# Weight casts moved in a decoder block: two gate units, two output units, one FFN unit, and two row blocks of the projection summed together

## The chip, the cores and the metric

The kernel runs on one core of a Trainium2 chip. Its time is the device time of one execution in microseconds (us). The engines are named as in the profile: PE (TensorE, matmuls), PEld (its weight loads), DVE (VectorE), ACT (ScalarE), POOL (GpSimd) and SP (SyncE, which here issues the DMAs).

## The reference

One decoder block on x of 1 x 1024 x 1024 floats: a projection, two attentions, gates, an output projection and a SwiGLU FFN of width 2816.

```python
h = rmsnorm(x, mix_norm_g[l])
proj = h @ w_in[l]
qa, ka, va, q_lat, kv_lat, k_r, g_a, g_b = jnp.split(proj, IN_OFFSETS, axis=-1)
...
o_a = swa_sink_attention(qa, ka, va, swa_sinks[l])      # 8 heads, window 128
...
o_b = mla_attention(q_nope, q_rope, k_nope, k_rope, vb) # 8 heads, causal
y = jax.nn.sigmoid(g_a) * (o_a @ w_o_swa[l]) + jax.nn.sigmoid(g_b) * (o_b @ w_o_mla[l])
x = x + y @ w_out[l]
h = rmsnorm(x, ffn_norm_g[l])
x = x + (jax.nn.silu(h @ w_gate[l]) * (h @ w_up[l])) @ w_down[l]
return rmsnorm(x, final_norm_g)
```

## The kernel before

Everything is single precision. A float operand is split in two parts: `split(hi, lo, src)` casts to the narrower type that PE takes (`hi`, on ACT, line 163) and subtracts it from the source (`lo`, on DVE, line 166). `mm3` then makes each product of three matmuls: high by high (line 172), high by low (173) and low by high (174). Nearly every weight passes through such a pair of a cast on ACT and a subtraction on DVE before PE can use it; `wl`, `wh` and `wv` are the names of split weights, `wr` of raw ones, and `pth`/`ptl`, `yh`/`yl`, `t3h`/`t3l` and so on those of split activations.

The stages that the change touches, in the order of the program:

- **Gates and local attention** (scores from 129 to 304 us). The two gate projections are computed by the class `Seven` in seven block products per pair of columns j, each for q in a fixed sequence; `gates.run()` runs the next unit (j, q), and `prep_to(n)` prepares units (additions on POOL, then the split of the weights, `wl`) until n are prepared, by default 3 ahead (`n_ahead`). The loop over `it` interleaves three gate units (`gate_step`) with one block of the sliding-window attention: `sw_qT` transposes and splits the queries (`qs`), `sw_scores` makes the scores (`sc`, lines 917 and 918), their maxima on DVE (921), and the exponentials on ACT (933); `sw_pT` and `sw_pv` multiply by the values (`o`, copied to `ot` at 964). `scale_gate` multiplies raw weights of later units by the norm's gain on ACT (837).
- **The mix** (`oB` from 564 to 610 us). For eight columns `DCS = (4, 5, 0, 1, 6, 7, 2, 3)`, `mix_b` makes `oB`, the product with `w_o_mla`, multiplies it by the gate and adds the other half: `sg<-oB,sg`, `sg<-sg,sg`, then the split into `yh` and `yl`. The weights come as units ("ob", 0..3) of two columns each, through a stream `st` of loads and conversions: `conv_to(i)` emits the conversions up to unit i (ACT `wh`, DVE `wl`). ("ob", 3) is used by columns 6 and 7, ("ob", 1) by 2 and 3.
- **The projection** (`xo`, from 610 us), a row block of 128 and 512 columns at a time: eight products of `y` with `w_out`, in the order of DCS, into one accumulator of the pool P1 (four banks).
- **The FFN's first units** (from about 705 us), again by `Seven`, with units for the gate (g) and the up projection (u); the tail of the projection's transposes (`late_parts`) lies between them.

What sets the order: PE and SP follow the written order in the gate stage and a scheduler orders ACT, DVE and POOL; in the mix the scheduler orders PE too, except that casts and sigmoids emitted while `held[0]` is set keep their place; from the last segment of the projection on, PE, DVE, ACT and POOL all follow the written order. Buffers are taken from pools in the order of emission.

Of the kernel before, what the change touches and what calls it, by code (L numbers as in the profile page):

```python
# [89 lines left out]
def hybrid_block_kernel(  # L90
# [49 lines left out]
    def uid(name):  # L140
        counter[0] += 1
        return f"{name}_{counter[0]}"
# [7 lines left out]
    def tiny(name, w=1):  # L150
        return small.tile([P, w], F32, tag=f"t{w}", name=uid(name))

    def P1(name, shape=(P, 512)):
        return ps1.tile(list(shape), F32, tag="ps", name=uid(name))

    def PX(name, shape=(P, 512)):
        return psum["x"].tile(list(shape), F32, tag="ps", name=uid(name))
# [10 lines left out]
    def mm3(ps, pairs, first=True, last=True, go_on=False):  # L168

        n = len(pairs)  # L170
        for i, ((ah, al), (bh, bl)) in enumerate(pairs):
            nc.tensor.matmul(ps, ah, bh, start=first and i == 0, stop=False, skip_group_check=go_on)  # L172
            nc.tensor.matmul(ps, ah, bl, start=False, stop=False, skip_group_check=go_on)  # L173
            nc.tensor.matmul(ps, al, bh, start=False, stop=last and i == n - 1, skip_group_check=go_on)  # L174
# [7 lines left out]
    def blk(b, n=1):  # L182
        return slice(b * P, (b + n) * P)
# [35 lines left out]
    st = Stream()  # L219
# [102 lines left out]
    def hT(k, sl):  # L322
        hi, lo = quad[(k // 4, sl.start // 512)]
        c = slice(sl.start % 512, (sl.stop - 1) % 512 + 1)
        return hi[:, k % 4, c], lo[:, k % 4, c]
# [193 lines left out]
    ps = kvq_ps[0] = PX("kvq")  # L519
# [337 lines left out]
    gates = Seven(NK, "g", load_gate, gate_done, 3, (1, 6), 5, scale=scale_gate, scale_at=[(2, 0, 0, 2), (7, 0, 2, 2), (7, 1, 0, 2), (5, 1, 2, 2)], piece=2, vec=(2, 5))  # L857
# [6 lines left out]
    for b in range(NB):  # L864
# [4 lines left out]
        ps = PX("ql", (P, 416))  # L869
# [35 lines left out]
    def sw_scores(it):  # L905
        g, b = divmod(it, NB)
        d = sw[it]
        qs = d.pop("qs")
        c0 = P if b == 0 else 0
        kc = slice((b - 1) * P + c0, (b + 1) * P)  # L910
        mx = tiny("mx", 4)
        scs = []
        for hp in range(2):
            sc = PX("sc", (P, 2, 2 * P))
            scs.append(sc)
            for j in range(2):
                nc.tensor.matmul(sc[:, j, c0:], qs[:, hp, j], khd[g][0][:, kc], start=True, stop=False)
                nc.tensor.matmul(sc[:, j, c0:], qs[:, hp, j], khd[g][1][:, kc], start=False, stop=True)
            for j in range(2):
                h = 2 * hp + j  # L920
                nc.vector.tensor_tensor_reduce(sc[:, j, c0:], sc[:, j, c0:], band[:, c0:], 1.0, NEG, op0=ALU.add,
                                               op1=ALU.max, accum_out=mx[:, h:h + 1])
        ns = nsink[:, 4 * g:4 * g + 4]
        nm = tiny("nm", 4)
        nc.vector.scalar_tensor_tensor(nm, mx, -SC_A, ns, op0=ALU.mult, op1=ALU.min)
        es = tiny("es", 4)
        nc.vector.tensor_tensor(es, nm, ns, op=ALU.subtract)
        den = tiny("den", 4)
        pe = U("pe", F32, (P, 4, 2 * P))
        for h in range(4):  # L930
            if h == 1:
                nc.scalar.activation(es, es, AF.Exp)
            nc.scalar.activation(pe[:, h, c0:], scs[h // 2][:, h % 2, c0:], AF.Exp, scale=SC_A, bias=nm[:, h:h + 1],
                                 accum_out=den[:, h:h + 1])
        nc.gpsimd.tensor_tensor(den, den, es, op=ALU.add)
        nc.gpsimd.tensor_tensor(den, den, neg_one, op=ALU.pow)
        for h in range(4):
            nc.gpsimd.tensor_scalar(pe[:, h, c0:], pe[:, h, c0:], den[:, h:h + 1], 0.0, op0=ALU.mult, op1=ALU.add)
        d["pe"] = pe
        d["kbs"] = [1] if b == 0 else [0, 1]  # L940
# [38 lines left out]
    for i, b in enumerate((4, 5, 6, 7, 0, 1, 2, 3)):  # L979
        ps = P1("kl", (P, KVL))  # L980
# [44 lines left out]
    for it in range(N_SW):  # L1025
        if it + 2 < N_SW:
            sw_q(it + 2)
        gate_step()
        if it + 1 < N_SW:
            sw_qT(it + 1)  # L1030
        gate_step()
        if it >= 1:
            sw_pv(it - 1)
        if it + 1 < N_SW:
            sw_scores(it + 1)
        if it == N_SW - 1:
            load_lat(4)
        gate_step()
        sw_pT(it)
# [125 lines left out]
    ob = {}  # L1165
# [145 lines left out]
    DCS = (4, 5, 0, 1, 6, 7, 2, 3)  # L1311
# [99 lines left out]
    def mix_b(dc, i):  # L1411
        if dc % 2 == 0:
            wo[4 + dc // 2] = st.get(("ob", dc // 2))
        w = wo[4 + dc // 2]
        ga, gb = gate.pop(dc), gate.pop(8 + dc)
        for sh in range(2):
            cs = half(sh)
            pb = PX("oB")
            mm3(pb, [((w[0][:, c, blk(dc % 2)], w[1][:, c, blk(dc % 2)]), obT[(c, sh)]) for c in range(4)])
            nc.vector.tensor_tensor(gb[:, cs], pb, gb[:, cs], op=ALU.mult)  # L1420
            if i == 7:
                add(ga[:, cs], ga[:, cs], gb[:, cs], nc.vector)
                split(*hT(dc, cs), ga[:, cs])
        for sh in range(2 if i < 7 else 0):
            cs = half(sh)
            add(ga[:, cs], ga[:, cs], gb[:, cs], nc.vector)
            split(*hT(dc, cs), ga[:, cs])

    def sigmoids(dc):
        for i in (dc, 8 + dc):  # L1430
            sigmoid(i)
        a_ = ar.pop(dc)
        for sh in range(2):
            nc.gpsimd.tensor_tensor(gate[dc][:, half(sh)], a_[:, half(sh)], gate[dc][:, half(sh)], op=ALU.mult)
# [9 lines left out]
    for i, dc in enumerate(DCS):  # L1444
        if i in (1, 2):
            st.load_to(st.index[("ob", (3, 1)[i - 1])])
        if 2 <= i < 6:
            st.load_to(st.index[("out", 0, OUT0[i - 2])])
        if i + 2 < 8:
            load_sigs(DCS[i + 2])  # L1450
        if rest:
            mix_a(*rest.pop(0), 0, 4, PX("oA"))
        if i + 1 < 8:
            sigmoids(DCS[i + 1])
        mix_b(dc, i)
        if i in (2, 3):
            st.conv_to(st.index[("ob", (3, 1)[i - 2])])
        if i >= 4:
            st.conv_to(st.index[("out", 0, OUT0[i - 4])])

# [60 lines left out]
    def ffn_done(j, m, ps, f, sh, other):  # L1521
# [8 lines left out]
        else:  # L1530
# [3 lines left out]
    ffn = Seven(HF, "gu", load_w, ffn_done, 4, (2, 7), 5, head,  # L1534
                {(1, 6): [("load", 2, 0)], (1, 7): [("load", 2, 1)], (1, 5): [("mix", 2)]})
# [75 lines left out]
    for seg, (sh, hf) in enumerate(((0, 0), (0, 1), (1, 1), (1, 0))):  # L1611
        if seg == 3:
            in_order.__enter__()
        if seg in (0, 1, 3):
            r = {0: 0, 1: 1, 3: 2}[seg]
            wo2 = [st.get(("out", r, j)) for j in range(4)]
        hs = half(hf)
        for b in range(4 * sh, 4 * sh + 4):
            if seg in (0, 2):
                x2[b] = load_x(b)  # L1620
            if (seg, b) == (2, 4):
                ffn.load_part(0, 0)
            if (seg, b) == (2, 6):
                ffn.load_part(0, 1)
            if (seg, b) == (2, 7):
                ffn.mix(0)
            ps = P1("xo")
            mm3(ps, [(hT(k, blk(b)), (wo2[k // 2][0][:, k % 2], wo2[k // 2][1][:, k % 2])) for k in DCS])
            add(x2[b][:, hs], ps, x2[b][:, hs], nc.vector)
            if seg in (0, 2):  # L1630
                st.conv_to(st.index[("out", seg // 2 + 1, b % 4)])
            if seg in (1, 3):
                xn = U("xn")
                ss = tiny("ss")
                nc.scalar.activation(xn, x2[b], AF.Square, accum_out=ss)  # L1635
                rs = rstd_of(ss, D)
            lower = to_h(*prev) if prev is not None else None
            prev = None
            if seg in (1, 3):
                nc.vector.scalar_tensor_tensor(xn, x2[b], rs, fg_bc, op0=ALU.mult, op1=ALU.mult)  # L1640
                prev = (xn, b)
                if (seg, b) == (3, 6):
                    ffn.prep_to(3)
                nc.sync.dma_start(x2_d[b], x2.pop(b))
            if (seg, b) == (3, 7):
                for kh in range(2):
                    ffn.load_part(1, kh)
            if lower is not None:
                if seg == 3 and b >= 6:
                    late_parts.append(lower)  # L1650
                else:
                    lower()
# [1 line left out]
    ffn.run()  # L1654
    late_parts.pop(0)()
    ffn.run()
    ffn.prep_to(4)
    late_parts.pop(0)()
    ffn.run()
    ffn.prep_to(6)  # L1660
# [89 lines left out]
    i = 0  # L1750
# [125 lines left out]
```

## Time and profile before

| | |
|---|---|
| median of 3 runs | 1345.6 us (1345.04 to 1346.36) |
| the profiled execution | 1345.58 us, its span 1343.8 us, mean granted clock 0.998 |
| PE busy | 1325.5 us, 99% of the span, 6564 matmuls |
| DVE, ACT, POOL busy | 67%, 47%, 42% |
| DMA | 223.61 MB, mean 166 GB/s |

In the rows of the timeline the columns are start, duration (both us), engine, line, operation, output <- inputs, sizes, and in brackets the idle time of the engine before the row and what released it. A matmul's duration overlaps that of the next one; the distance between starts is what one costs. In the table of waits a row reads: engine, tile and line that waited <- engine, tile and line that released it, then the total, the number of times and the longest.

### The profile page before, as it was taken

How to read it: one execution, taken by the hardware profiler on the slowest of the kernel's cores; microseconds unless marked ns; L12 is line 12 of the kernel's file. 1: busy time of each engine (PE TensorE's matmuls, PEld its weight loads, DVE VectorE, ACT ScalarE, POOL GpSimd, SP SyncE). 2: the span in 40 equal slices, each digit the busy share in tenths (PEclk: the TensorE clock that was granted, in tenths of full speed). 3: DMA queues.
4: the chain of work that ended last, by engine and by line, in shares of the span. 5: the costliest groups of instructions: out<-in, count | busy, mean ns of one | idle time of the engine just before them, and what ended most of it. 6: DMA issues, size and time to landing. Idle time of an engine off the chain costs nothing. (4 is left out here: it accounts for less than half of the span.)

```text
span 1343.8 us, 19035 instructions
## 1 busy us (share of the span) xinstructions
PE 1325.5 (99%) x6564; PEld 1115.0 (83%) x6564; DVE 903.5 (67%) x1471; ACT 635.7 (47%) x1291; POOL 567.6 (42%) x614
## 2 busy tenths in 40 slices
PE   9999999999999999999999999999999999999997
PEld 6899878888888889877887888888888888888886
DVE  7868777776767667696458775566665664764862
ACT  7434767665556767762436223232223232644343
POOL 2116646553224554451031665756666541022521
PEclk9999999999999999999999999999999999999999
DMA  9454322335476430771432454545544425996504
GB/s 374 152 188 156 118 97 83 109 124 187 155 243 160 107 99 17 264 268 48 190 140 96 166 175 146 203 162 180 177 141 153 164 96 194 383 373 238 173 13 144
DMA packets 85311, 223.61 MB, mean 166 GB/s; under 512 B 9632, under 2 KB 16288, under 8 KB 84128
## 3 DMA queue, kind: packets, MB, share of 16 engines
q1 hardware_dynamic: 83776, 220.05, 47.5%
q10 hardware_dynamic: 1440, 2.36, 0.5%
q8 instruction: 52, 0.85, 0.3%
q14 instruction: 43, 0.35, 0.1%
HBM read 151.72 MB, written 70.12 MB: 165 GB/s over the span
## 5 line engine op out<-in xcount | busy, mean ns | idle before, releaser
L166 DVE TENSOR_TENSOR wl<-wr,wl 128x512 fp32r<-128x512 f32 x150 | 150.8, 1029 | 72.6 <-ACT wl L163 72.2
L166 DVE TENSOR_TENSOR lrv<-lr,lrv 128x1024 fp32r<-128x1024 f32 x77 | 105.1, 1396 | 49.3 <-ACT lrv L163 45.3
L163 ACT CAST lrv<-lr 128x1024 fp32r<-128x1024 f32 x77 | 80.1, 1052 | 95.7 <-PE fd L174 69.8
L172 PE MATMUL fd<-lrv 128*128 128x512 f32 x308 | 119.8, 389 | 0.0
L173 PE MATMUL fd<-lrv 128*128 128x512 f32 x308 | 119.8, 389 | 0.0
L174 PE MATMUL fd<-lrv 128*128 128x512 f32 x308 | 119.8, 389 | 0.0
L177 POOL TENSOR_TENSOR wr<-wr,sm 128x512 f32<-128x512 f32 (+1 forms) x38 | 46.2, 1225 | 145.4 <-DVE wl L166 114.2
L163 ACT CAST wl<-wr 128x512 fp32r<-128x512 f32 x150 | 86.9, 622 | 1.9 <-DVE wr L835 1.7
L1198 POOL TENSOR_TENSOR denb<-denb,neg_one 128x1 f32<-128x1 f32 x64 | 40.1, 626 | 96.2 <-ACT p L1197 84.1
L166 DVE TENSOR_TENSOR wl<-sm,wl 128x512 fp32r<-128x512 f32 x60 | 48.7, 837 | 46.3 <-ACT wl L163 46.2
L311 POOL TENSOR_SCALAR ms<-ss 128x1 f32<-128x1 f32 x32 | 9.4, 292 | 143.7 <-ACT xn L1635 67.5
L173 PEld LDWEIGHTS fd<-lrv 128*128 128x128 f32 x308 | 57.8, 188 | 12.1
L174 PEld LDWEIGHTS fd<-lrv 128*128 128x128 f32 x308 | 57.8, 188 | 12.0
L172 PEld LDWEIGHTS fd<-lrv 128*128 128x128 f32 x308 | 57.8, 188 | 11.9
L1197 ACT ACTIVATE p<-scb,nmb 128x384 f32<-128x384 f32 (+3 forms) x64 | 47.8, 747 | 33.3 <-DVE nmb L1196 25.6
L166 DVE TENSOR_TENSOR ptl<-pTb,pth 128x512 fp32r<-128x512 f32 (+2 forms) x96 | 50.5, 552 | 16.6 <-ACT pth L163 16.3
L1196 DVE CUSTOM_DVE_ANT_0 scb<-scb,mask 128x384 f32<-128x384 f32 (+3 forms) x64 | 48.6, 761 | 15.0 <-PE scb L1188 13.0
L1529 ACT ACTIVATE act<-sm 128x512 f32<-128x512 f32 x11 | 7.0, 633 | 104.8 <-DVE sm L180 104.8
L1199 POOL TENSOR_SCALAR p<-p,denb 128x384 f32<-128x384 f32 (+3 forms) x64 | 47.9, 748 | 6.3
L172 PE MATMUL xo<-wv,yh 128*128 128x512 f32 x120 | 47.4, 395 | 1.2 <-ACT yh L163 1.2
L1529 ACT ACTIVATE act<-pu 128x512 f32<-128x512 f32 x22 | 13.9, 633 | 71.0 <-DVE pu L180 71.0
L163 ACT CAST pth<-pTb 128x512 fp32r<-128x512 f32 (+2 forms) x96 | 43.4, 482 | 8.5 <-PE pTb L1213 7.5
(356 smaller groups left out, 4315.1 us busy)
## 6 DMA issues: line engine op xcount, KB each, us to landing
lr<-la_d SPq DMA_DIRECT2D x77, 256.0 KB, 5.4
wr<-in_w_gate_dram SPq DMA_DIRECT2D x22, 512.0 KB, 4.4
wr<-in_w_up_dram SPq DMA_DIRECT2D x22, 512.0 KB, 5.1
wd<-in_w_down_dram SPq DMA_DIRECT2D x22, 512.0 KB, 7.1
rb_d<-wd SPq DMA_DIRECT2D x22, 512.0 KB, 2.7
la_d<-sd SPq DMA_DIRECT2D x22, 512.0 KB, 5.9
lr<-rb_d SPq DMA_DIRECT2D x44, 256.0 KB, 5.4
lr<-in_w_down_dram SPq DMA_DIRECT2D x33, 256.0 KB, 5.4
```

The costliest lines, as they stand in the source:

```text
L163: i = nc.scalar.copy(hi, src)
L166: (eng or nc.vector).tensor_tensor(lo, src, hi.bitcast(F32), op=ALU.subtract)
L172: nc.tensor.matmul(ps, ah, bh, start=first and i == 0, stop=False, skip_group_check=go_on)
L173: nc.tensor.matmul(ps, ah, bl, start=False, stop=False, skip_group_check=go_on)
L174: nc.tensor.matmul(ps, al, bh, start=False, stop=last and i == n - 1, skip_group_check=go_on)
L177: eng.tensor_tensor(out, a, b, op=ALU.subtract)
L311: nc.gpsimd.tensor_scalar(ms, ss, 1.0 / width, EPS, op0=ALU.mult, op1=ALU.add)
L1196: nc.vector.tensor_tensor_reduce(s_, s_, m_, 1.0, -NEG, op0=ALU.add, op1=ALU.min, accum_out=nm)
L1197: nc.scalar.activation(p_, s_, AF.Exp, scale=-1.0, bias=nm, accum_out=den)
L1198: nc.gpsimd.tensor_tensor(den, den, neg_one[:, 0:1], op=ALU.pow)
L1199: nc.gpsimd.tensor_scalar(p[:, 0:w], p[:, 0:w], den, 0.0, op0=ALU.mult, op1=ALU.add)
L1529: nc.scalar.activation(dst, src, AF.Silu)
```

## The change

Four edits. In the loop of the local attention, when the next gate unit to run is (2, 1) or (5, 1), the gates are prepared up to three units ahead already before `sw_scores`. The conversions of ("ob", 3) and ("ob", 1) are called ahead of `mix_b` at i = 2 and 4, instead of behind it at i = 2 and 3. In the projection the first two row blocks take an accumulator each and sum the first six columns of DCS for both, then the last two columns for both. And `ffn.prep_to(4)` becomes `prep_to(5)`.

```diff
         if it + 1 < N_SW:
+            if gates.seq[gates.n_run][:2] in ((2, 1), (5, 1)):
+                gates.prep_to(gates.n_run + 3)
             sw_scores(it + 1)
...
             sigmoids(DCS[i + 1])
+        if i in (2, 4):
+            st.conv_to(st.index[("ob", (3, 1)[i // 2 - 1])])
         mix_b(dc, i)
-        if i in (2, 3):
-            st.conv_to(st.index[("ob", (3, 1)[i - 2])])
...
-            ps = P1("xo")
-            mm3(ps, [(hT(k, blk(b)), (wo2[k // 2][0][:, k % 2], wo2[k // 2][1][:, k % 2])) for k in DCS])
+            if seg == 0 and b < 2:
+                if b == 0:
+                    xo2 = [P1("xo") for _ in range(2)]
+                    for ks in (DCS[:6], DCS[6:]):
+                        for u in range(2):
+                            mm3(xo2[u], [(hT(k, blk(u)), (wo2[k // 2][0][:, k % 2], wo2[k // 2][1][:, k % 2])) for k in ks],
+                                ks[0] == DCS[0], ks[0] != DCS[0])
+                ps = xo2[b]
+            else:
+                ps = P1("xo")
+                mm3(ps, [(hT(k, blk(b)), (wo2[k // 2][0][:, k % 2], wo2[k // 2][1][:, k % 2])) for k in DCS])
...
-    ffn.prep_to(4)
+    ffn.prep_to(5)
```

ACT at the first of the two gate places, before; the first `wl` row is the cast of unit (2, 2), `pe` are the exponentials, `pth` the split of the transposed probabilities:

```order
L964 COPY ot_2304<-o_2299 64x512
L933 ACTIVATE pe_2329,den_2328<-sc_2310,nm_2324 128x256
L932 ACTIVATE es_2326<-es_2326 128x4
L933 ACTIVATE pe_2329,den_2328<-sc_2310,nm_2324 128x256
L933 ACTIVATE pe_2329,den_2328<-sc_2317,nm_2324 128x256 x2
L163 COPY wl_2341<-wr_2089 128x512
L163 COPY pth_2362<-pT_2364 128x512
L163 COPY pth_2362<-pT_2371 128x512
L163 COPY wl_2382<-wr_2025 128x512
L899 COPY qs_2404<-qT_2401 64x2x128
```

And after:

```order
L964 COPY ot_2304<-o_2299 64x512
L163 COPY wl_2309<-wr_2089 128x512
L933 ACTIVATE pe_2332,den_2331<-sc_2313,nm_2327 128x256
L932 ACTIVATE es_2329<-es_2329 128x4
L933 ACTIVATE pe_2332,den_2331<-sc_2313,nm_2327 128x256
L933 ACTIVATE pe_2332,den_2331<-sc_2320,nm_2327 128x256 x2
L163 COPY pth_2362<-pT_2364 128x512
L163 COPY pth_2362<-pT_2371 128x512
L163 COPY wl_2382<-wr_2025 128x512
L837 ACTIVATE wr_2344<-wr_2344,gT 128x256
L899 COPY qs_2404<-qT_2401 64x2x128
```

The cast now stands ahead of the exponentials, and one gain multiplication (837) ahead of `qs`. Behind these rows two more gain multiplications have moved ahead of the next copy to `ot`. On DVE the low half of the cast moved ahead of three of the four maxima.

ACT in the mix, before; `wh_6812` is the cast of unit ("ob", 1), `wv` are casts of `w_out`:

```order
L1269 ACTIVATE sg_6724<-sg_6724 128x1024
L163 COPY yh_6608<-sg_6674 128x512
L163 COPY wh_6812<-wr_6718 128x1024
L163 COPY wv_6911<-wr_6768 128x1024
L1269 ACTIVATE sg_6770<-sg_6770 128x1024
L1269 ACTIVATE sg_6772<-sg_6772 128x1024
L163 COPY yh_6610<-sg_6722 128x512
L163 COPY yh_6612<-sg_6722 128x512
L163 COPY wv_6952<-wr_6816 128x1024
L1269 ACTIVATE sg_6818<-sg_6818 128x1024
```

And after, where the same cast is called `wh_6824`:

```order
L1271 ACTIVATE sg_6724<-sg_6724 128x1024
L163 COPY yh_6608<-sg_6674 128x512
L163 COPY wv_6911<-wr_6768 128x1024
L1271 ACTIVATE sg_6770<-sg_6770 128x1024
L1271 ACTIVATE sg_6772<-sg_6772 128x1024
L163 COPY yh_6610<-sg_6722 128x512
L163 COPY yh_6612<-sg_6722 128x512
L163 COPY wv_6952<-wr_6812 128x1024
L163 COPY wh_6824<-wr_6718 128x1024
L1271 ACTIVATE sg_6814<-sg_6814 128x1024
```

The cast of unit 1 moved behind two sigmoids, two `yh` and a `wv`. That of unit 3, a few rows earlier, stands in the same place in both programs, and so do its low half on DVE and its matmuls on PE.

PE at the first matmuls that use unit 1, after; before, the rows of `oB_6918` ran through without a break:

```order
L172 MATMUL oB_6918<-obT_6206,wh_6824 128x512
L173 MATMUL oB_6918<-obT_6206,wh_6824 128x512
L172 MATMUL oB_6932<-obT_6206,wh_6824 128x512
L173 MATMUL oB_6932<-obT_6206,wh_6824 128x512
L172 MATMUL oB_6955<-obT_6206,wh_6824 128x512
L173 MATMUL oB_6955<-obT_6206,wh_6824 128x512
L172 MATMUL xo_6998<-wv_6862,yh_6610 128x512
L173 MATMUL xo_6998<-wv_6862,yh_6610 128x512
L174 MATMUL xo_6998<-wv_6862,yl_6611 128x512
L172 MATMUL xo_6998<-wv_6862,yh_6610 128x512
L174 MATMUL oB_6918<-obT_6206,wl_6825 128x512
```

Ahead of the first matmul that needs the low half (`wl_6825`) now stand two matmuls of each of three columns' halves and four of the projection.

In the FFN, ACT and DVE follow the written order: the first of the two casts that stood behind the activation (line 1529) now stands directly behind the cast of the unit before it, ahead of `b22h`, `t3h`, the table load and the activation.

## The prediction

> **What bounds the kernel now.** I read the page's busy times first, then the table of waits for TensorE, then the timeline around each wait.
>
> ```profile
> span 1343.8 us, 19035 instructions
> PE 1325.5 (99%) x6564; PEld 1115.0 (83%) x6564; DVE 903.5 (67%) x1471; ACT 635.7 (47%) x1291; POOL 567.6 (42%) x614
> ```
>
> PE is busy for 99% of the span and the change removes no matmul, so all there is to win or lose is PE's idle time. The profiled execution took 1345.58 us, the span and 1.8 us around it; the median of the runs is 1345.6, so I sum against 1345.58. About 0.2%, 2.7 us, is what a measurement of this kernel can tell from no change. The waits of PE (total, times, longest):
>
> ```profile
> PE fa L172 <- ACT wl L163: 3.3, 3, 1.5
> PE xo L172 <- ACT yh L163: 1.2, 1, 1.2
> PE oB L172 <- ACT wh L163: 0.9, 1, 0.9
> PE oB L174 <- DVE wl L166: 0.9, 1, 0.9
> ```
>
> Each edit is aimed at one of these: the gates at two of the three `fa` waits, ffn.prep_to(5) at the third, the projection at `xo`, the earlier `ob` conversion at `oB`. They sum to 6.3 us, 0.5% of the time. A wait costs more than its row. The timeline at the first gate wait shows it:
>
> ```profile
> 196.25 0.39 PE L896 MATMUL qT<-ident,qn 128*128 128x128 f32 x2
> 197.68 0.50 PE L172 MATMUL fa<-hh,wl 128*128 128x512 f32 x1 [1.04 <-ACT wl L163]
> ...
> 198.74 0.39 PE L172 MATMUL fa<-hh,wl 128*128 128x512 f32 x1
> ...
> 596.56 0.39 PE L172 MATMUL oB<-obT,wh 128*128 128x512 f32 x1
> ...
> 599.28 0.39 PE L172 MATMUL oB<-obT,wh 128*128 128x512 f32 x1
> ```
>
> The last two rows are twelve undisturbed `oB` matmuls apart: 2.72/12 = 0.227 us each. From 197.68 to 198.74 PE starts three matmuls in 1.06 instead of 0.68 us: a tail of 0.38. The two transposes at 196.25 take some 0.23, so PE could have gone on at about 196.48: idle 1.2, and 1.58 with the tail.
>
> **The gates.** ACT and DVE around that wait:
>
> ```profile
> 195.09 0.47 ACT L933 ACTIVATE pe<-sc,nm 128x256 f32<-128x256 f32 x1 [3.66 <-DVE nm L925]
> 197.00 0.62 ACT L163 CAST wl<-wr 128x512 fp32r<-128x512 f32 x1
> 202.64 0.59 ACT L964 COPY ot<-o 64x512 f32<-64x512 f32 x1
> 207.62 0.63 ACT L163 CAST wl<-wr 128x512 fp32r<-128x512 f32 x1
> 197.66 0.69 DVE L166 TENSOR_TENSOR wl<-wr,wl 128x512 fp32r<-128x512 f32 x1 [1.80 <-ACT wl L163]
> 201.45 0.42 DVE L902 TENSOR_TENSOR qs<-qT,qs 64x256 fp32r<-64x256 f32 x1
> 208.28 0.69 DVE L166 TENSOR_TENSOR wl<-wr,wl 128x512 fp32r<-128x512 f32 x1 [1.76 <-ACT wl L163]
> 201.72 0.28 PE L917 MATMUL sc<-khd,qs 128*128 128x256 f32 x1
> 209.33 0.47 PE L172 MATMUL fb<-t4h,wl 128*128 128x512 f32 x1
> ```
>
> ACT sat idle for 3.66 us ahead of its exponentials (195.09), and the cast (197.00) stood behind them. In the new order it stands ahead of them, so the wait goes: +1.58. What it adds: DVE's low half of the cast (0.69) now lies ahead of the maxima, so the exponentials start some 0.6 later, near 195.7. The scheduler also puts one gate-gain ACTIVATE ahead of `qs` and two of the next four ahead of the copy to `ot`; four take 1.70 us in one row:
>
> ```profile
> 200.30 1.70 ACT L837 ACTIVATE wr<-wr,gT 128x256 f32<-128x256 f32 x4
> ```
>
> so 0.43 each. The scores (201.72) need `qs`, whose last DVE half starts at 201.45 and whose first comes 0.45 sooner; nothing in the DVE order makes it earlier by more than 0.4. PE would now reach the scores at 201.72 - 1.58 = 200.14 and find the first half done at about 201.1 to 201.5. It waits 1.0 to 1.4 there: 0.2 to 0.6 of the 1.58 is left. Then `ot` (202.64) moves back by about 1.0 (three ACTIVATEs, less the cast that went ahead), the second maxima, exponentials and the cast behind them (207.62, its low half 208.28 to 208.97) with it, against a slack of 0.36 at 209.33. PE waits again, 0.4 to 0.7 with a tail. I take +0.3 us slower for this gate. The second gate has the same rows 79 us later:
>
> ```profile
> 276.76 0.50 PE L172 MATMUL fa<-hh,wl 128*128 128x512 f32 x1 [0.76 <-ACT wl L163]
> ```
>
> with 0.76 of idle by the row, and 0.54 more if the first gate's 1.58 for a row of 1.04 is a guide, so 1.3; by the same steps, 0.2 slower. Both: +0.5 us, from -2.9 (both waits go, nothing new) to +1.2.
>
> **The oB weights.** Rows of the two units whose conversion is moved:
>
> ```profile
> 587.09 0.50 PE L172 MATMUL oB<-obT,wh 128*128 128x512 f32 x1 [0.94 <-ACT wh L163]
> 589.40 0.50 PE L174 MATMUL oB<-obT,wl 128*128 128x512 f32 x1 [0.89 <-DVE wl L166]
> 592.47 1.05 ACT L163 CAST wh<-wr 128x1024 fp32r<-128x1024 f32 x1
> 599.67 0.63 ACT L163 CAST yh<-sg 128x512 fp32r<-128x512 f32 x1 [1.03 <-DVE sg L180]
> 600.20 1.04 ACT L163 CAST wv<-wr 128x1024 fp32r<-128x1024 f32 x1
> 588.13 1.22 DVE L166 TENSOR_TENSOR wl<-wr,wh 128x1024 fp32r<-128x1024 f32 x1
> 594.52 1.72 DVE L166 TENSOR_TENSOR wl<-wr,wh 128x1024 fp32r<-128x1024 f32 x1
> ```
>
> For unit 3 (wait 587.09 and 589.40) the new order of ACT, DVE and PE is the old one there, so these 1.8 us stay. For unit 1 the cast `wh`, at 592.47 before, is emitted one column later, and ACT's order puts it behind two `yh` and a `wv` (the second `yh` at 599.67, `wv` at 600.20). The `yh` wait for DVE's sums, which the edit does not hasten, so `wh` follows `wv` at about 601.2 and, with its 1.05, ends at 602.2. PE wants it at 599.28, the first matmul of the columns 2 and 3. New wait: 602.25 - 599.28 = 2.97, with a tail of 0.38 about 3.4. The low half (1.22 and 1.72 in its two rows) ends near 604.4 to 604.9; PE's new order fills in six `oB` and four `xo` matmuls (10 x 0.227 + 0.38 = 2.65, to 604.9), so it adds 0 to 0.4. Behind `wh` queue two sigmoids and the next `yh`; POOL and DVE wait for those, PE only later.
>
> **The projection.** The first row block waits for the last column:
>
> ```profile
> 616.32 0.50 PE L172 MATMUL xo<-wv,yh 128*128 128x512 f32 x1 [1.24 <-ACT yh L163]
> 615.65 0.62 ACT L163 CAST yh<-sg 128x512 fp32r<-128x512 f32 x1 [1.84 <-DVE sg L180]
> ```
>
> 1.24 by the row, and 0.54 more as at the gates: 1.78. Now the first six columns of two row blocks come first, so 36 matmuls, 32 of them (7.3 us) behind the oB matmuls, stand before the one that needs the last `yh` (cast at 615.65). That wait goes: -1.78. The number of matmuls is unchanged, and two accumulators of four are in use. SP's order is the same, and its late loads feed weights that are used tens of us later. Weights and projection: 3.4 - 1.8 = +1.6 us, from -1.8 (unit 1 hidden) to +2.2.
>
> **The FFN.** Rows around the third `fa` wait:
>
> ```profile
> 718.77 0.50 PE L172 MATMUL fa<-b11h,wl 128*128 128x512 f32 x1 [1.46 <-ACT wl L163]
> 715.20 0.59 ACT L1500 CAST b22h<-tp 128x512 fp32r<-128x512 f32 x1 [1.36 <-DVE t L177]
> 718.11 1.13 ACT L163 CAST wl<-wr 128x512 fp32r<-128x512 f32 x2
> 722.63 0.62 ACT L163 CAST wl<-wr 128x512 fp32r<-128x512 f32 x1
> 715.08 1.41 DVE L177 TENSOR_TENSOR t2l<-t,t2h 128x512 fp32r<-128x512 f32 x1
> 724.62 0.39 PE L172 MATMUL fa<-b21h,wl 128*128 128x512 f32 x1
> ```
>
> The wait is 1.46 by its row, and 0.54 more as at the gates: 2.0. Of the two casts at 718.11 (the gate's unit and the up projection's) the first moves ahead of 715.20, where ACT was idle for 1.36 by that row. Its low half pushes DVE's and ACT's chain back by about 0.6. Then PE arrives 2.0 earlier at the next units. The up unit's cast comes just in time or 0.3 late. The unit after it has its cast at 722.63 behind a chain of transposes, not moved: PE, which reached it at 724.62 before, reaches it at 722.6 and waits until 723.3, 0.7 and a tail: 1.1. Left: 2.0 - 1.1 - 0.2 = 0.7. In this stretch DVE's `t2l` (715.08) took 1.41, where the same shape at the gates took 0.69; POOL works beside it. If the moved low half takes that long, the up unit is 0.7 later and the gain is nil; I take 0.7 since only one of the rows in that stretch is long, and keep 0 to 2.0.
> [...]
>
> **The sum.** +0.5 + 1.6 - 0.7 = +1.4: 1345.58 + 1.4 = 1347.0 us.
>
> **The rivals.** (1) The waits simply go. For it: each cast moves into a row of ACT idle time. Against it: the next consumer of each stage is 0.4 to 1.6 us behind. Gates -2.9, FFN -2.0, weights and projection +1.6: -3.3, 1342.3; if unit 1 is hidden too, -6.7, 1338.9. Chance 0.13.
> (2) Slower: the late `wh` cast of unit 1 decides alone. Every microsecond by which it ends after 602.2 is one more of PE's. The rows at 588.13 and 594.52 show one DVE form at 1.22 and, beside POOL's multiplications, 1.72; three such stretches ahead of the second `yh` end `wh` at 603.7, the wait is 4.9 instead of 3.4, and if the FFN gives nothing the sum is +0.5 + 4.9 - 1.8 = +3.6, 1349.2. It decides from a `wh` end of about 602.8, where the sum passes +2.7 without the FFN's gain. Chance 0.17.
> (3) A wait of 3 us drops PE's clock: rows show only the short tail for waits up to 1.5, none of 3. Were matmuls at half rate for as long as the wait, 3.4/0.45 = 7.5 of them would each cost 0.227 more: +1.7, in all +3.1, 1348.7. Chance 0.06. [...]
> (4) The change does not do what it says: the scheduler has already kept unit 3's cast in its place; if it hides unit 1's as well through timing that the order does not show, and gates and FFN cancel, only the projection is left: -1.8, 1343.8. Chance 0.08.
> My forecast has 0.56.
>
> **Chances and range.** Over 0.2% faster: (1), 0.13. Over 0.2% slower: (2), (3) and the upper end of the forecast: 0.24. Within: 0.63. The range takes the forecast's unknowns (-2.6 to +3.3) takes in the near case of (1) and (2): 1342.2 to 1349.3. Left out are the far case of (1) and ends beyond (2).
>
> **What would show it.** Right: PE waits at `oB` L172 for ACT `wh` twice, the new one 2.5 to 3.5 us; no `xo` wait for `yh`; new short waits at `sc` L917 and at the `fb` and `fa` units behind the moved ones. Wrong: no new `oB` wait, or `fa` waits under 0.5 us in all with no `sc` wait in their place; either would take 2 to 3 us off.

## The result and the profile after

The changed kernel takes 1348.99 us (median of 7 runs, 1348.29 to 1350.26), the kernel before 1345.04 in the runs beside it (7 runs, 1344.72 to 1348.04). The ratio is 1.0027, with a 95% interval of 1.0015 to 1.0038: slower by 2.0 to 5.1 us. Predicted were 1347.0 us and a range of 1342.2 to 1349.3. The profiled execution took 1350.21 us. Its span and busy times on the page:

```profile
span 1348.4 us, 19047 instructions
PE 1330.3 (99%) x6564; PEld 1116.7 (83%) x6564; DVE 903.6 (67%) x1471; ACT 635.6 (47%) x1291; POOL 569.8 (42%) x614
```

The same 6564 matmuls take 4.8 us more of PE time, and the span is 4.6 longer: what was lost is not idle time of PE alone, since matmuls themselves have become slower somewhere. The table of PE's waits after the change:

```profile
PE oB L172 <- ACT wh L163: 3.7, 2, 2.8
PE sc L917 <- DVE qs L901: 1.6, 2, 0.8
...
PE oB L174 <- DVE wl L166: 0.9, 1, 0.9
...
PE fa L172 <- ACT pu L812: 0.2, 1, 0.2
PE fa L172 <- ACT wl L163: 0.2, 1, 0.2
```

The three `fa` waits of before (3.3 in all) have shrunk to two of 0.2, and the `xo` wait (1.2) is gone. In their place stand two waits of 0.8 at the scores, and a second `oB` wait for ACT's `wh`, of 2.8. The waits that the change touches sum to 6.3 us before and to 6.6 after. So 4.6 us of span are not to be found in this table.

To place them, each PE matmul's start in a profile is set against the start of the same matmul in the profile of before. This **shift**, its median over stretches of 20 us, changes only where time is lost or won. From the changed kernel's start to its end it goes 0, 2.3 (from 20 us on), 2.1 (from 150 us on, still ahead of the first edit), 2.7 (behind the two gates), 5.4 (behind the mix and the projection), 4.6 (behind the FFN's first units, and to the end).

**The first 2.1 us** are not the change's: up to there the two programs have the same instructions in the same order. The first projection's 16 matmuls in the timeline of before, and of after:

```profile
5.72 7.10 PE L522 MATMUL kvq<-wr,h 128*128 128x512 f32 x16 [1.11 <-DMA wr<-in_w_x_dram]
```

```profile
5.43 9.70 PE L522 MATMUL kvq<-wr,h 128*128 128x512 f32 x16 [0.60 <-DMA wr<-in_w_x_dram]
```

They take 9.70 instead of 7.10 us. The trace's record of PE's clock reaches full speed 4.27 us into the span of before, and 10.64 us into that of after. Among the profiles of the other kernels below it is 5.1 to 5.4 or 9.9 to 10.4 with the same instructions at the start (4.27 in one), so executions that begin alike differ in this; by the shift of 2.1 it can scatter the times of single runs by about 2 us, an estimate. The shift at a place is free of it. What the change did is therefore 4.6 - 2.1 = 2.5 us in the traces, and the interval of the times, 2.0 to 5.1, holds that.

**The mix: a new wait, and half a clock behind it.** PE's timeline of after at the first matmuls with unit 1's weights:

```profile
601.75 0.39 PE L174 MATMUL oB<-obT,wl 128*128 128x512 f32 x1
604.93 0.79 PE L172 MATMUL oB<-obT,wh 128*128 128x512 f32 x1 [2.79 <-ACT wh L163]
605.52 0.63 PE L173 MATMUL oB<-obT,wh 128*128 128x512 f32 x1
605.95 0.63 PE L172 MATMUL oB<-obT,wh 128*128 128x512 f32 x1
...
607.65 0.55 PE L172 MATMUL xo<-wv,yh 128*128 128x512 f32 x1
```

and ACT's just before, then the windows of the same stretch (columns: window in us, its length, busy us and instructions of PE, PEld, DVE, ACT and POOL, granted clock of PE, DMA share, GB/s):

```profile
601.82 1.17 ACT L163 CAST yh<-sg 128x512 fp32r<-128x512 f32 x2 [3.98 <-DVE sg L180]
602.89 1.04 ACT L163 CAST wv<-wr 128x1024 fp32r<-128x1024 f32 x1
603.84 1.04 ACT L163 CAST wh<-wr 128x1024 fp32r<-128x1024 f32 x1
```

```profile
602.00:605.00 3.00, 0.21 (x2) 0.07 (x1) 3.00 (x6) 3.00 (x5) 0.00 (x0) 0.93 0.87 269
604.90:608.00 3.10, 3.07 (x7) 2.48 (x8) 3.10 (x4) 2.39 (x3) 2.09 (x1) 0.50 0.85 280
608.00:612.00 4.00, 4.00 (x19) 3.30 (x18) 3.22 (x4) 1.57 (x3) 1.85 (x2) 1.00 0.86 331
```

ACT's `wh` stands behind `yh`, `yh` and `wv`, and the first of those waits 3.98 us for DVE's sums, as was worked out. PE starts nothing from 601.75 to 604.93: 3.18 us, of which 0.227 are the last matmul's, so 2.95 are lost. Then the starts are 0.43 apart (605.52, 605.95) instead of 0.227, up to 607.65; the granted clock is 0.50 in that window and 1.00 in the next. The clock record has 0.5 for 3.41 us, from 604.56 to 607.97. Of that, 3.04 us lie behind the wait. From 604.93 to the full clock the matmuls' starts take 1.5 us more than 0.227 us each would: half of the 3.04. That is where PE's busy time grew while the table of waits stayed as long.

**The gates.** ACT, DVE and PE at the first gate, by start:

```profile
193.45 0.62 ACT L163 CAST wl<-wr 128x512 fp32r<-128x512 f32 x1
197.95 0.47 ACT L933 ACTIVATE pe<-sc,nm 128x256 f32<-128x256 f32 x1 [3.88 <-DVE nm L925]
...
201.33 0.55 ACT L837 ACTIVATE wr<-wr,gT 128x256 f32<-128x256 f32 x1
201.74 0.37 ACT L899 CAST qs<-qT 64x256 fp32r<-64x256 f32 x1
...
203.10 0.42 DVE L901 TENSOR_TENSOR qs<-qT,qs 64x256 fp32r<-64x256 f32 x1
...
203.57 0.39 PE L917 MATMUL sc<-khd,qs 128*128 128x256 f32 x1 [0.80 <-DVE qs L901]
...
211.44 0.50 PE L172 MATMUL fb<-t4h,wl 128*128 128x512 f32 x1
211.78 0.40 PE L173 MATMUL fb<-t4l,wl 128*128 128x512 f32 x1
212.17 0.50 PE L174 MATMUL fb<-t4h,wl 128*128 128x512 f32 x1
```

The cast `wl` is at 193.45, ahead of the exponentials (197.95) as the order has it, and PE runs through the unit that waited before. Behind it a gain ACTIVATE (201.33) stands ahead of `qs` (201.74), DVE's first low half of `qs` starts at 203.10, and PE waits 0.80 at the scores. At the `fb` unit behind them PE is just held up: no wait is listed, but the starts are 0.34 and 0.39 apart (211.44, 211.78, 212.17), a slow tail as behind the gate wait of before (0.38). The second gate has the same rows 79.5 us later.

**The FFN.** PE at the two `fa` rows that wait now:

```profile
728.27 0.50 PE L172 MATMUL fa<-b21h,wl 128*128 128x512 f32 x1 [0.15 <-ACT wl L163]
731.74 0.50 PE L172 MATMUL fa<-b21h,wl 128*128 128x512 f32 x1 [0.19 <-ACT pu L812]
```

The 1.46 of before has gone, and 0.15 and 0.19 have come at the units behind it.

### The profile page after: what moved, and what is told of

It reads as the page before. It is cut to its first block, busy times and chain, and to the rows that moved or that the text cites. A ratio compares the mean times of both kernels' runs of the same rounds, so it can differ in the third digit from the quotient of the medians.

```text
span 1348.4 us, 19047 instructions
## 1 busy us (share of the span) xinstructions
PE 1330.3 (99%) x6564; PEld 1116.7 (83%) x6564; DVE 903.6 (67%) x1471; ACT 635.6 (47%) x1291; POOL 569.8 (42%) x614
## 5 line engine op out<-in xcount | busy, mean ns | idle before, releaser
L173 PE MATMUL fd<-lrv 128*128 128x512 f32 x308 | 119.8, 389 | 0.0
L173 PEld LDWEIGHTS fd<-lrv 128*128 128x128 f32 x308 | 57.8, 188 | 12.0
L172 PE MATMUL fb<-t2h,wl 128*128 128x512 f32 x120 | 47.4, 395 | 0.0
```

## The experiments

In the table is what each kernel's trace shows at the places of the change, as the growth of the shift there (us, + is slower), and its time against the kernel before on the same chip. The start's clock moves single runs by about 2 us and scatters the medians, so the shifts tell the theories apart, and the ratios say whether the times agree.

| kernel | gates | mix and projection | FFN | sum | ratio [95%] |
|---|---|---|---|---|---|
| changed kernel | +0.6 | +2.7 | -0.8 | +2.5 | 1.0027 [1.0015, 1.0038] |
| the same again | +0.6 | +2.7 | -0.8 | +2.5 | 1.0021 [1.0012, 1.0029] |
| gates alone | +0.6 | | | +0.6 | 1.0008 [0.9999, 1.0017] |
| `ob` alone | | +2.9 | | +2.9 | 1.0016 [1.0006, 1.0027] |
| projection alone | | -1.8 | | -1.8 | 0.9990 [0.9981, 0.9999] |
| FFN alone | | | -0.8 | -0.8 | 0.9998 [0.9989, 1.0007] |
| `ob` and projection | | +2.8 | | +2.8 | 1.0016 [1.0007, 1.0025] |
| all but `ob` | +0.6 | -1.8 | -0.8 | -2.0 | 0.9996 [0.9987, 1.0005] |
| unit 3 earlier | | +1.1 | | +1.1 | 1.0007 [0.9998, 1.0016] |
| gates, high half only | -0.1 | | | -0.1 | 1.0006 [0.9997, 1.0015] |
| best of the parts | | -4.2 | -0.8 | -5.0 | 0.9963 [0.9951, 0.9975] |

The shifts scatter a little too. At 332 us the shift falls by 0.1 in all thirteen profiles, with the gates' edit or without it; the gates' column holds that fall, so that the edit of the gates costs 0.7 rather than 0.6. At 720 us it falls by 0.2 in five kernels whose FFN is as before, where the cell is empty. One loss lies outside the places of the change: in the profiles of the gates alone and of all but `ob`, PE waits at 1144.87 and 1141.55 us for DVE's `lrv`, a split weight of the last product (0.38 and 0.44 by the rows, at `fd` L173), behind a cast that waited for its load of `w_down`, and the shift grows by 0.7 and 0.8. No other profile has this wait, and one profile of each kernel can't say whether an edit brings it.

**Each edit by itself.** The first four kernels are the kernel before with one of the four edits, each as it stands in the diff of the change.

The gates alone:

> Only the edit of the gates. Theory (the cast's low half on DVE delays the exponentials, so the wait moves to the scores and then to the next cast): both `fa` waits for `wl` at the gates go, waits at `sc` L917 for `qs` of about 0.8 each come, total +0.6 us (0 to +1.2). Rival (the waits simply go): -2.9 us, no `sc` wait.

Measured: 1347.01 us (11 runs) beside 1345.93 for the kernel before. Its waits:

```profile
PE sc L917 <- DVE qs L901: 1.7, 2, 0.8
...
PE fa L172 <- ACT wl L163: 1.2, 1, 1.2
```

Of three `fa` waits one is left, the FFN's, and the two `sc` waits are there without any other edit. The gates cost 0.6 us by the table: the gain was handed on to the scores and to the `fb` unit behind them, and lost there with a little on top.

The conversions of `ob` alone:

> Only the edit of the ob conversions. Theory (unit 1's cast is late by 3 us and PE's clock is halved behind the wait): a wait at `oB` L172 of 2.8 us, matmuls at 0.43 instead of 0.227 us for about 3.4 us behind it, the `xo` wait stays, total +4.7 us. Rival (the half clock in the changed kernel's profile was an accident of one execution): +3.0 to +3.4. Rival (the wait is hidden by the projection's own wait): +1.6.

Measured: 1347.83 us (11 runs). Its waits at these places:

```profile
PE oB L172 <- ACT wh L163: 3.7, 2, 2.8
...
PE oB L174 <- DVE wl L166: 0.9, 1, 0.9
```

The new wait of 2.8 and 3.41 us at half clock (602.41 to 605.82) come from this edit alone. Here the half clock lies behind the wait as a whole and costs 1.7 us. The loss at unit 1 is 4.7 us as expected, but the sum is +2.9, since no `xo` wait is left in this kernel either, whose projection is as before. PE comes late to the projection by 4.7 us, with four of its matmuls already done in the gap, and DVE and ACT, which did not wait, have the last `yh` ready. That gives 1.8 back.

The projection alone:

> Only the two row blocks of the projection summed together. Theory: the `xo` wait for `yh` of 1.24 and its tail go and nothing comes in its place, -1.8 us. Rival (the last columns are late for the second half too): 0 to -0.5.

Measured: 1344.75 us (11 runs), -1.8 in the trace; the `xo` wait is gone, and nothing comes in its place.

The FFN alone:

> Only ffn.prep_to(5). Theory: the `fa` wait of 1.5 goes with its tail (-2.0), two short ones of 0.2 and 0.3 to 0.5 of idle with tails come behind it, -0.8 us. Rival (the wait simply goes): -2.0. Rival (the next unit's cast takes it all): 0.

Measured: 1345.99 us (11 runs), -0.8 in the trace. One line of its waits has moved in size:

```profile
PE fa L172 <- ACT wl L163: 2.0, 3, 1.0
```

Before, the three were 3.3, with 1.5 the longest. The time itself can't tell this from no change (interval 0.9989 to 1.0007).

**Does a wait halve the clock, and for how long?** Two kernels lengthen a wait that is already there, the projection's for the last column's `yh`, by doing that column's cast on ACT again, to the same place (N = 2 and N = 4 times, for the first half of the last column):

```diff
+                for _ in range(N if sh == 0 else 0):
+                    nc.scalar.copy(hT(dc, cs)[0], ga[:, cs])
                 split(...)
```

Casts done three times in all:

> The kernel before, with the cast of the last column that the projection waits for made three times instead of once (same values), to lengthen that wait from 1.24 to about 2.3 us. Theory (PE's clock is halved for 3.41 us by an idle time of about 3 us, and not by a shorter one): no half clock at 616, PE loses 1.1 more and no more. Rival (any wait over 2 us does it): half clock, 1.1 + 1.6 more.

Five times in all:

> The same with the cast made five times, the wait about 4 to 5 us. Theory: the clock record shows 0.5 for 3.41 us around the end of the wait, some 7 matmuls at 0.43 us, so PE loses the added wait and 1.6 more. Rival (the half clock lasts as long as the wait, as the prediction's third rival assumed): 4 to 5 us of it, 2.0 to 2.4 more. Rival (the half clock at `oB` has another cause): none.

Measured, in one run each: 1348.06 and 1349.96 us. PE at the wait of the first, with the window that holds the wait and the two behind it (these windows list of the engines PE alone, then the clock and the DMA):

```profile
618.78 0.50 PE L172 MATMUL xo<-wv,yh 128*128 128x512 f32 x1 [2.52 <-ACT yh L163]
```

```profile
615.00:618.00 3.00, 1.26 (x6) 1.00 0.00 0
618.00:621.00 3.00, 2.22 (x8) 1.00 0.00 0
621.00:624.00 3.00, 3.00 (x15) 1.00 0.00 0
```

and of the second:

```profile
619.11 0.79 PE L172 MATMUL xo<-wv,yh 128*128 128x512 f32 x1 [5.04 <-ACT yh L163]
619.70 0.63 PE L173 MATMUL xo<-wv,yh 128*128 128x512 f32 x1
620.12 0.63 PE L174 MATMUL xo<-wv,yl 128*128 128x512 f32 x1
```

```profile
615.00:618.00 3.00, 0.00 (x0) 0.70 0.00 0
618.00:621.00 3.00, 1.89 (x5) 0.50 0.00 0
621.00:624.00 3.00, 3.00 (x10) 0.66 0.00 0
```

The clock is 1.00 through and behind the wait of 2.52, and the shift grows by 1.3, the added wait and no more. With 5.04 it falls to half inside the wait, 2.3 us after PE went idle, and stays there for 6.83 us, where the changed kernel had 3.41; the starts are 0.43 apart (619.70, 620.12), and the shift grows by 5.4: 3.8 of added wait (5.04 less 1.24) and 1.6. The wait of before already had a tail of 0.38, so the matmuls at half clock behind the wait cost 2.0 us in all, half of the 3.94 us from the wait's end to the full clock at 623.05. So at the same place, with no other change to the kernel, the wait of 5.04 brought the half clock and that of 2.52 did not, in one profile each. Neither expected length holds as put: the record isn't one 3.41 whatever the wait, and not as long as the wait. The expected 1.6 beyond the added wait came out.

**Mending the `oB` edit.** Unit 3 is converted one column earlier than before, behind `mix_b` at i = 1, and unit 1 stays at i = 3; the other edits are left out:

```diff
         mix_b(dc, i)
-        if i in (2, 3):
-            st.conv_to(st.index[("ob", (3, 1)[i - 2])])
+        if i in (1, 3):
+            st.conv_to(st.index[("ob", (3, 1)[i // 2])])
```

> The kernel before, with the conversions of unit 3 and unit 1 called behind mix_b at i = 1 and 3 (before: 2 and 3), so that unit 3 really moves ahead. Theory: both `oB` waits at unit 3 (0.94 and 0.89, with tails 2.4) go, unit 1 stays without a wait, -2.4 us. Rival (the sums on DVE are late then and the projection's wait grows by the same): 0 to -1.

Measured: 1346.41 us (11 runs) beside 1345.31. Both `oB` waits are gone, 2.4 us with their tails. But the head of its table of waits, and PE at that place:

```profile
PE xo L172 <- ACT yh L163: 3.2, 1, 3.2
PE fa L172 <- ACT wl L163: 3.1, 3, 1.2
```

```profile
614.98 0.50 PE L172 MATMUL xo<-wv,yh 128*128 128x512 f32 x1 [3.17 <-ACT yh L163]
...
616.27 0.56 PE L173 MATMUL xo<-wv,yh 128*128 128x512 f32 x1
616.63 0.63 PE L174 MATMUL xo<-wv,yl 128*128 128x512 f32 x1
```

PE reaches the projection sooner, waits there for the last `yh` for 3.17 instead of 1.24, and the clock falls to half 1.4 us after the wait has ended (616.34 to 619.75 by the record). All that was won is lost again, and 1.1 more. An edit that gains 2.4 by itself needs the projection edit beside it.

**Mending the gates.** Only ACT's cast goes ahead of the maxima, and DVE's low half is held back behind them, by keeping it in program order behind the subtraction that ends them:

```diff
+            if getattr(self, "late", None) is None:
                 split(t[:, 0], t[:, 1], src)
+            else:
+                nc.scalar.copy(t[:, 0], src)
+                self.late.append((t[:, 1], src, t[:, 0].bitcast(F32)))
...
             sw_scores(it + 1)
+            for lo, src, hi in getattr(gates, "late", None) or ():
+                tc.keep_in_program_order(nc.vector.tensor_tensor(lo, src, hi, op=ALU.subtract))
```

> The edit of the gates, with only the cast (ACT) ahead of the scores and its low half (DVE) held behind the maxima. Theory (it is the low half on DVE that delays exponentials, probabilities and `qs`): the `sc` waits shrink from 0.8 to 0.2 or 0.3 each, total -0.6 us against before, 1.2 better than the gates' edit. Rival (the gain multiplications on ACT ahead of `qs` and `ot`, of which three stand there now, decide): waits of 0.8 or more stay, total +0.6 or more.

Measured: 1346.45 us (11 runs), -0.1 in the trace over the two gates together. ACT and DVE at the first:

```profile
200.50 1.31 ACT L841 ACTIVATE wr<-wr,gT 128x256 f32<-128x256 f32 x3
201.72 0.35 ACT L903 CAST qs<-qT 64x256 fp32r<-64x256 f32 x1
202.07 0.37 ACT L904 CAST qs<-qT 64x256 fp32r<-64x256 f32 x1
...
202.47 0.42 DVE L905 TENSOR_TENSOR qs<-qT,qs 64x256 fp32r<-64x256 f32 x1 [0.52 <-ACT qs L904]
```

The exponentials are no longer late, but the scheduler now puts three gain ACTIVATEs (1.31 us at 200.50) ahead of the two `qs` casts, so DVE's `qs` waits for ACT (0.52) and PE for DVE, as the row in its table of waits says:

```profile
PE sc L921 <- DVE qs L905: 1.0, 2, 0.6
```

The low half's delay was a part of the loss; the multiplications that take the freed place on ACT now stand in its stead.

**The sum of the parts.** The changed kernel again, the changed kernel with the `ob` edit undone, the `ob` and projection edits together, and a kernel put together from what was learnt: the projection and FFN edits of the change with unit 3 converted one column earlier, and the gates as before.

> The changed kernel once more. Theory: the `oB` wait for `wh` of 2.8 and the half clock behind it come again, as in its first profile and in that of the ob edit alone; by the sum of the sites +2.5 against before (+0.8 where the half clock stays away, +4.6 where PE's clock also comes up late at the start and the run of before has it early). Rival (the half clock is rare): about +0.8 in most runs.

Measured: 1348.51 us (12 runs) beside 1345.45, the same shifts, the same 2.8-us wait, and half clock from 603.77 to 607.18.

> The changed kernel with the ob conversions put back where they were. Theory (the ob edit is the whole loss; the three others sum to +0.6, -1.8 and -0.8): -2.0 us against before, no `oB` wait at unit 1, no half clock. Rival (the projection edit gives only 0.2, as beside the ob edit): -0.4.

Measured: 1345.46 us (11 runs); -2.0 in the trace at the places of the change, and no half clock. The ratio doesn't tell it from no change (-1.7 to +0.7 us), and -2.0 lies just outside that. With the late wait for `lrv` named above (+0.8) the trace has -1.2 to its end, which lies inside. At the places of the change the kernel without the `ob` edit is 4.5 us better than with it; by the medians of the same session it is 3.1 better (1345.46 and 1348.51).

> The ob edit and the projection edit. Theory (the late unit 1 already puts the projection's wait out of the way, so the two are not additive): +2.7 us, within 0.3 of the ob edit alone by the trace. Rival (additive: the ob edit's +2.9 and the projection's -1.8): +1.1.

Measured: 1347.71 us (11 runs); +2.8, where the `ob` edit alone has +2.9. Beside it the projection edit, worth 1.8 alone, is worth nothing: the late unit has put its wait away already.

> The projection edit, ffn.prep_to(5), and unit 3 converted one column earlier (unit 1 where it was); no gates' edit. Theory (the early unit 3 takes away the two `oB` waits, and the wait of 3.2 that it caused at the projection falls away since the last columns are summed last): -2.4 - 1.8 - 0.8 = -5.0 us, no half clock. Rival (the last columns come too late even so): a wait at `xo`, -1 to -3.

Measured: 1340.24 us (5 runs, 1339.95 to 1342.46) beside 1345.45, ratio 0.9963 [0.9951, 0.9975]: 3.4 to 6.6 us faster than the kernel before, and faster than the changed one. The trace has -2.4 at unit 3, -1.8 at the projection and -0.8 in the FFN. Its windows over the mix and the projection:

```profile
580.00:600.00 20.00, 20.00 (x90) 16.57 (x89) 18.83 (x22) 13.81 (x17) 9.13 (x6) 1.00 0.88 322
600.00:612.00 12.00, 12.00 (x55) 9.93 (x54) 12.00 (x15) 6.15 (x9) 4.87 (x3) 1.00 0.79 261
612.00:622.00 10.00, 10.00 (x46) 8.29 (x45) 8.38 (x12) 4.65 (x7) 3.44 (x2) 1.00 0.00 0
```

PE is busy in all 42 us at full clock.

## Why the prediction was right, and the term it lacked

- **The gates**: +0.5 forecast, +0.6 in four traces (0.7 without the fall at 332 us). The wait moved to the scores' `qs`, 0.80 by its row at each gate where 1.0 to 1.4 was worked out for the first, and a second hold came at the `fb` unit, where a wait of 0.4 to 0.7 with its tail was taken: a tail alone, 0.39 us, with no idle time listed.
- **Unit 3**: its waits stay, 0.96 and 0.88 us in after; both programs have the same order there.
- **Unit 1**: the mechanism and the wait were right, 2.95 lost between starts where 2.97 was the estimate. The term that was mis-sized is what comes behind it. The sum had a tail of 0.38, from waits up to 1.5 us; there came 1.5 at half clock. This was rival (3), at a chance of 0.06. The rows at hand had no wait longer than 1.5, so that they could not speak against it. The trace of before did show what a longer one does, at its end: the last matmul starts at 1336.39, PE has nothing more to do, and the clock record falls to half at 1338.88, when PE had been idle for 2.3 us, less than the 2.97 that were forecast. The rival deserved more. Its half rate was the author's assumption, and the window of after shows 0.50. Its "for as long as the wait" no run shows: half clock lasted 3.41 us with the wait of 2.79 and 6.83 with the one of 5.04. And its amount was too large: 1.7 on top of the tail, where 1.5 came in place of it.
- **The projection**: -1.8 was right for the edit by itself. Beside the `ob` edit it gives nothing, and the two terms were summed as if independent. The sum is not hurt by that: the old `xo` wait goes once, whichever edit removes it, and 2.95 + 1.5 - 1.8 = 2.65 is the 2.7 of the trace.
- **The FFN**: -0.7 forecast, -0.8 in five traces. Of the 2.0 won, 1.3 were to come back (1.1 and 0.2), and 1.2 did, as two waits of 0.15 and 0.19 with their tails, one of them for `pu` and not for a cast. The moved low half took 0.68 us (from 719.60), though POOL's multiplication began at 719.76; the row that is longer beside POOL is again `t2l`, with 1.19. So the 1.41, at which the gain would have been nil, did not come at the moved low half.
- **The sum**: +1.4 forecast, +2.5 in the traces, and the half clock, 1.5 where a tail of 0.38 was taken, accounts for that difference of 1.1. The medians are 4.0 apart, or +3.6 [2.0, 5.1] by the ratio; a repeat gave +2.8 [1.6, 3.9], and both intervals hold the 2.5. That the median, 1348.99, lies in the range is in part luck: it is 0.3 below the upper end, and that end was worked out for rival (2), which did not happen, and not for the half clock. The likeliest outcome by the forecast, within 0.2% of before, is missed by the ratio's middle (0.27%), though its interval begins at 0.15%.

The rivals: (1) and (4) fell, since the new waits are there; (2) fell, since `wh` ended at 604.88 with the shift of 2.7 taken off at 602.2, the forecast's own figure; (3) happened, with a smaller amount.

## What to carry to other kernels

Before a conversion is moved, write down what stands ahead of it on its engine in the new order, since "sooner" in the code was later on ACT. Two edits that remove waits within a few microseconds of each other are to be priced together: a delay upstream can hide a wait downstream (`ob` beside the projection), and a gain upstream can lengthen it (unit 3 earlier without the projection edit). And a new wait on PE is to be priced with the matmuls at half clock that may follow: here 1.5 to 1.7 us behind the waits of 2.8 at unit 1, 2.0 behind the one of 5.04, and none behind the one of 2.52.

## What the runs showed of the hardware

**Half clock at some waits.** Each figure here is of one profile. The wait for `wh` at unit 1 came with half clock in the four kernels that have it: by its rows it was 2.79 us in the changed kernel and in the same again, 2.77 in `ob` alone, and 2.80 in `ob` with projection. The wait for `yh` came with it at 3.17 (unit 3 earlier) and at 5.04 (fivefold cast), and not at 2.52 (threefold cast) or at the 1.24 of before. The record has 0.5 for 3.41 us in the changed kernel, the same again, `ob` alone and unit 3 earlier, and for 6.83 us in the fivefold cast. Where it begins differs: 2.9 us ahead of the wait's end in the fivefold cast (616.22 and 619.11), 0.37 ahead of it in the changed kernel (604.56 and 604.93), 0.59 behind it in `ob` alone (602.41 and 601.82), and 1.36 behind it in unit 3 earlier (616.34 and 614.98). The length of a wait alone does not sort the cases: at the end of before the clock fell when PE had been idle for 2.27 us, and the wait of the threefold cast, 2.68 between starts, left it alone. What else decides was not shown.

**A start that varies.** Full clock came 4.3 to 5.4 us into the span in some executions and 9.9 to 10.6 in others of the same instructions, worth about 2 us by the shift (2.1 in the changed kernel), nearly as much as the change does. With differences of 0.2%, shifts between traces told more than medians of 11 runs.
